# Delta-rule scan, then gated linear attention, each with projections between its steps, and softmax attention alone on four PSUM banks

## The chip, the cores and the metric

One core of a Trainium2 chip runs the whole kernel. The metric is device time in microseconds (us) of one execution.

## The reference, cut to what matters

Two layers of a latent-diffusion trunk on 512 latent and 256 context tokens (768 together), 1024 channels, fp32. In each layer three groups of heads read one input projection and write into one output projection, and a gated convolution FFN follows:

```python
pc = jnp.split(hc @ w_in, IN_SPLITS, axis=-1)
px = jnp.split(hx @ w_in, IN_SPLITS, axis=-1)
qn_x, qr_x, kn_x, kr_x, v_x = mla_project(px, mla_q_norm, mla_w_uq, mla_kv_norm, mla_w_ukv)
...
mla_x = mla_attention_blocked(qn_x, qr_x, cat(kn_c, kn_x), cat(kr_c, kr_x), cat(v_c, v_x))
gdn_c, gdn_x = bidirectional_scan(gated_delta_chunked, seq_c, dir_c, seq_x, dir_x, ...)
gla_c, gla_x = bidirectional_scan(gla_chunked, sq_c, dr_c, sq_x, dr_x, ...)
y_x = merge_heads(mla_x, gdn_x, z_x, gdn_norm, gla_x, gg_x, gla_norm) @ w_out
```

- MLA: softmax attention with 8 heads over keys and values that are projected up from a small rank.
- GDN, the gated delta rule: chunks of 64 tokens one after the other, 12 in each direction, with a state S per head. A step computes `v_new = u - w @ S`, `o = qd @ S + A @ v_new`, `S = S * glast + kend.T @ v_new`.
- GLA, gated linear attention: a short recurrence over chunk states, then an output for each chunk.

The second layer has no output for the context tokens.

## The kernel before, in words

fp32 products of the large matrices run as three products of high and low parts (`fprod`, `fsteps`, line 221: one step is three matmuls). Each engine's instructions have a fixed order, which the framework's scheduler writes when the kernel is built, from the order in which the Python code emits them. PSUM has eight banks: two tiles `bb` of two banks each (projections, scores of attention) and four single banks with the tags a, b, c and d. `ab("bc")` (line 183) hands out banks b and c in turn; `ab()` goes by `self.tags`. A tile of a bank must be read out before the next tile of that bank is written.

A layer emits, in this order (`layer`, line 310):

1. `project_in`: the part of w_in that GDN needs, and the preparation of each 128-token tile (`gdn_prep`, `gdn_tile`), with projection steps between, taken from a generator by `pace(n)` (line 232).
2. `gdn_scan` (line 970): 12 steps, both directions in one step. A step on TensorE: `kq` (keys and queries times the state Sb, 16 matmul records in the trace, line 990), then `vp` (line 1004), `up` (the update of the state, one bank for each direction, line 1015), `op` (line 1034). Between them on VectorE: r (996, 997), vs (1008), the four adds to Sb (1022), tq (1026), the output (1038 or 1041); vn on ScalarE (1029); Sb times its decay on GpSimd (1018). In steps 2, 3 and 8 to 11, where the other direction has already passed the chunk, the output of two chunks is complete, and `head_out` (line 1069) norms, transposes and gates it. All of it takes banks b and c in turn. `pace(8)` runs twice in a step, behind r and behind vp; the filler is the rest of the projections (`projections`: GLA's keys, queries and values, MLA's inputs, the gate), and its single banks are a and d. ada, the conditioning matmuls of the FFN's modulation, come from a background list.
3. `mla_project` (line 1251): keys, queries and V of MLA, banks a and d; then head pair 0 of attention.
4. `gla` (line 1085), banks c and d: the chunk states of both directions, seven levels for each segment of tokens (inside a chunk, lines 1187 to 1217), and an output for each 128-token tile (lines 1219 to 1248) with `head_out`. Context first, then latent; layer 1 needs no context output.
5. Attention of pairs 1 to 3 (line 1350), banks a and b. A tile of 128 queries and two heads: scores into `bb`, maximum (1377, VectorE), exponential (1380, ScalarE), transposes of P into single banks, copies out (1392, 1394), product with V in a single bank.
6. `w_out`, whose first matmuls need GLA's and GDN's rows of the mix (stored in `md`, read back at line 356), then the FFN.

The scheduler lets stages overlap in each engine's order as far as banks, buffers and data allow: before, attention's pair 0 runs while the scan ends, and GLA and attention's pairs run side by side.

Of the kernel before, what the change touches and what calls it, by code (L numbers as in the profile page):

```python
# [11 lines left out]
F32 = mybir.dt.float32  # L12
# [29 lines left out]
SN = (8, 8)  # L42
# [4 lines left out]
WO = ((4, 5, 6, 7, 0, 1, 2, 3), (4, 5, 6, 7, 0, 1, 2, 3))  # L47
SPF = 0
# [87 lines left out]
class Net:  # L136
# [40 lines left out]
    def s1(self, pool=None):  # L177
        return (pool or self.B).tile([128, 256], F32, name=self.nm("s"), tag="s", bufs=4 if pool is None else 6)
# [53 lines left out]
    def pace(self, n):  # L232

        while n and self.fill:
            try:
                next(self.fill[0])
                n -= 1
            except StopIteration:
                self.fill.pop(0)

# [70 lines left out]
    def layer(self, l, later):  # L311
# [16 lines left out]
        self.krope = self.dram([128, T], "krope")  # L328
        Fp, self.F = self.pool("F", "right")
        Cp, self.C = self.pool("C", "right")  # L330
        F1p, self.F1 = self.pool("F1", "right")
        F2p, self.F2 = self.pool("F2", "right")
# [4 lines left out]
        Ap, self.A = self.pool("A")  # L337
        A0p, self.A0 = self.pool("A0")
        A1p, A1 = self.pool("A1")
        with self.ahead(HM):  # L340
            self.mla_project(A1)
# [19 lines left out]
        self.tags = "ab"  # L361
# [191 lines left out]
    def project_in(self, later):  # L553
# [62 lines left out]
        def gdn(m):  # L616
            dst = dsts[m]
            for i in range(2):
# [3 lines left out]
                for a, b in segs:  # L622
# [7 lines left out]
                    if m != 1:  # L630
                        sq = self.F2.tile([128, 512], F32, name=self.nm("sq"), tag="sq", bufs=2)
# [7 lines left out]
        self.cq, self.ckv = [], []  # L639
        self.rr = self.small(12, "rr", 2)  # L640
# [48 lines left out]
        def projections():  # L689
# [3 lines left out]
            yield from gla_v()  # L693
            yield from mla_in(0)
            if not last:
                yield from mla_in(1)
            yield from gate(1)
# [22 lines left out]
        self.tags = "ad"  # L720
        self.gdn_scan()
        self.fill = []
        drain(rest)
# [246 lines left out]
    def gdn_scan(self):  # L970
# [7 lines left out]
        def s1():  # L978
            return self.s1(self.C)

        for n in range(12):
# [24 lines left out]
            self.pace(SN[1])  # L1006
            vs = s1()
            nc.vector.tensor_tensor(vs.rearrange(h4, h=4), vp[:, :256].rearrange(h4, h=4),
                                    self.eks[:, n].unsqueeze(2).to_broadcast(b4), op=ALU.mult)
            for d in range(2):  # L1010
                t, hf = ch[d] // 2, ch[d] % 2
                up = self.ab("bc")
# [10 lines left out]
            if need_o:  # L1023
                m = (3 if n < 4 else 15) - n
                vn, tq = s1(), s1()
                nc.vector.tensor_tensor(tq.rearrange(h4, h=4), ks[:, 256:].rearrange(h4, h=4), eg, op=ALU.mult)
                if m < n:
                    nc.gpsimd.tensor_tensor(tq, tq, ost[m], op=ALU.add)
                nc.scalar.copy(vn, vp[:, :256])
                op = self.ab("bc")  # L1030
                for h in range(4):
                    for d in range(2):
                        e = d * 4 + h
                        self.mm(op[half[d], h * 64:(h + 1) * 64], self.AT[ch[d] // 2][half[d], e * 64:(e + 1) * 64],
                                vn[half[d], h * 64:(h + 1) * 64], True, True)
                if m > n:
                    ost[n] = self.C.tile([128, 256], F32, name=self.nm("ost"), tag="ost", bufs=4)
                    nc.vector.tensor_tensor(ost[n], tq, op[:, :256], op=ALU.add)
                    continue

                nc.vector.tensor_tensor(tq, tq, op[:, :256], op=ALU.add)
                if n % 2 == 0:
                    lo = min(n, m) - 1
                    pieces = [(lo * 64, lo * 64 + 256)] if n < 10 else [(256, 384), (640, 768)]
                    zt = self.gates(0, pieces)
                first = (4 if n >= 10 else lo) if n % 2 == 0 else first
                pos = [c - first if c - first < 4 else c - first - 4 for c in (n, m)]
                self.head_out(tq, zt, [64 * pos[(hf - n) % 2] for hf in range(2)], 0)
                if n % 2:
                    self.ungates(zt, 0, pieces)  # L1050
# [16 lines left out]
    def head_out(self, o, zt, cols, i):  # L1067
# [8 lines left out]
        ps = self.ab("cd" if i else "bc")  # L1076
# [8 lines left out]
    def gla(self):  # L1085
# [11 lines left out]
        for a, b in (CS, XS):  # L1097
# [34 lines left out]
            for d in range(2):  # L1132
# [22 lines left out]
                for st in steps:  # L1155
# [30 lines left out]
            for li, w in enumerate((32, 16, 8, 4, 2, 1, 0)):  # L1186
# [21 lines left out]
                for x in range(2):  # L1208
# [3 lines left out]
                    for i in range(nt):  # L1212
                        for c in range(2):
# [3 lines left out]
                                              ps[:, :nt * 128].rearrange("p (e j) -> p e j", j=64))  # L1217

            for i in range(nt):
                t, sl = t0 + i, slice(i * 128, (i + 1) * 128)  # L1220
                pieces = [(a + i // 2 * 256, a + i // 2 * 256 + 256)]
                if i % 2 == 0:
                    zt = self.gates(1, pieces)
# [22 lines left out]
                self.head_out(o, zt, [p0, p0 + 64], 1)  # L1246
                if i % 2:
                    self.ungates(zt, 1, pieces)


    def mla_project(self, A1):
# [38 lines left out]
        for e in range(2):  # L1290
            rope = at("tab", 1)
            nc.sync.dma_start(rope, self.a["rope"][e])
            for p in range(4):
                wh, wl = self.wsplit(self.a["w_uq"][l, 2 * p + e], 384)
                ps = self.bb()
                self.fprod(ps, wh, wl, cqh, cql, self.osegs, 3)
# [10 lines left out]
        for t in range(6):  # L1307
# [8 lines left out]
            self.V.append(v)  # L1316

# [248 lines left out]
```

## Time and profile before

| | us |
|---|---|
| median of three runs | 2274.95 (2271.13 to 2276.51) |
| the profiled execution | 2278.35 |
| its span, first to last instruction | 2276.6 |
| TensorE busy in the span | 2045.0 (90%) |
| VectorE, ScalarE, GpSimd busy | 1310.4, 1008.7, 536.0 |
| granted TensorE clock, mean | 0.934 |

The median is the metric. The rows below are of the profiled execution, so a sum made from them is to be set against 2278.35 us. A granted clock of 1 is 2.4 GHz for TensorE, and half of it is 1.2 GHz; a mean of 0.934 says that TensorE ran at the lower level for a part of the time.

### The profile page before, as it was taken

How to read it: one execution, taken by the hardware profiler on the slowest of the kernel's cores; microseconds unless marked ns; L12 is line 12 of the kernel's file. 1: busy time of each engine (PE TensorE's matmuls, PEld its weight loads, DVE VectorE, ACT ScalarE, POOL GpSimd, SP SyncE). 2: the span in 40 equal slices, each digit the busy share in tenths (PEclk: the TensorE clock that was granted, in tenths of full speed). 3: DMA queues.
4: the chain of work that ended last, by engine and by line, in shares of the span. 5: the costliest groups of instructions: out<-in, count | busy, mean ns of one | idle time of the engine just before them, and what ended most of it. 6: DMA issues, size and time to landing. Idle time of an engine off the chain costs nothing. (4 is left out here: it accounts for less than half of the span.)

```text
span 2276.6 us, 44601 instructions
## 1 busy us (share of the span) xinstructions
PE 2045.0 (90%) x18168; PEld 1672.8 (73%) x18168; DVE 1310.4 (58%) x2474; ACT 1008.7 (44%) x1928; POOL 536.0 (24%) x897
## 2 busy tenths in 40 slices
PE   7898999888888799999999969988988777999996
PEld 4677777765667578888888857876766567888886
DVE  3354535668845743354454686556667757655556
ACT  4553323565464633332232456633446446543333
POOL 1342121135502310000010143413122613211102
PEclk8799999998898999999999979999989988999997
DMA  6232345422042354422212333111412053323322
GB/s 262 67 118 100 109 148 164 143 66 68 13 149 92 121 179 167 157 103 65 66 57 66 102 109 124 61 44 62 155 43 96 6 171 102 111 94 96 99 94 92
DMA packets 85134, 235.64 MB, mean 104 GB/s; under 512 B 9088, under 2 KB 24896, under 8 KB 84928
## 3 DMA queue, kind: packets, MB, share of 16 engines
q1 hardware_dynamic: 84928, 232.78, 30.7%
q8 instruction: 143, 2.34, 0.4%
q14 instruction: 63, 0.52, 0.1%
HBM read 204.04 MB, written 28.70 MB: 102 GB/s over the span
## 5 line engine op out<-in xcount | busy, mean ns | idle before, releaser
L212 PE MATMUL bb<-hh,wl 128*128 128x512 f32 (+1 forms) x1520 | 548.3, 361 | 18.0 <-DVE wl L192 10.9
L212 PE MATMUL bb<-hl,wh 128*128 128x512 f32 (+1 forms) x1520 | 542.0, 357 | 5.8 <-POOL hl L550 4.4
L192 DVE TENSOR_TENSOR wl<-wr,wh 128x512 fp32r<-128x512 f32 (+2 forms) x452 | 338.3, 751 | 362.3 <-ACT wh L191 361.0
L212 PE MATMUL bb<-hh,wh 128*128 128x512 f32 (+1 forms) x1520 | 540.2, 355 | 0.0
L191 ACT CAST wh<-wr 128x512 fp32r<-128x512 f32 (+2 forms) x452 | 274.1, 611 | 518.0 <-PE bb L212 370.3
L212 PEld LDWEIGHTS bb<-hh,wl 128*128 128x128 f32 x1520 | 293.2, 193 | 75.2 <-DVE wl L192 14.0
L212 PEld LDWEIGHTS bb<-hl,wh 128*128 128x128 f32 x1520 | 292.8, 193 | 49.4 <-POOL hl L550 7.8
L212 PEld LDWEIGHTS bb<-hh,wh 128*128 128x128 f32 x1520 | 292.9, 193 | 39.6 <-issue 2.1
L212 PE MATMUL bb<-g,wh 128*128 128x512 f32 (+1 forms) x1024 | 263.7, 349 | 2.3 <-DVE g L192 2.3
L1441 POOL TENSOR_SCALAR y<-u,fmt 128x512 f32<-128x512 f32 (+2 forms) x88 | 80.6, 917 | 527.1 <-ACT u L824 525.6
L212 PEld LDWEIGHTS bb<-g,wh 128*128 128x128 f32 x1024 | 181.5, 195 | 27.5 <-DVE g L192 3.3
L212 PE MATMUL bb<-g,wl 128*128 128x512 f32 (+1 forms) x512 | 180.3, 354 | 21.4 <-DVE wl L192 8.5
L212 PEld LDWEIGHTS bb<-g,wl 128*128 128x128 f32 x512 | 99.2, 195 | 36.9 <-ACT g L191 9.3
L824 ACT ACTIVATE u<-bb,fmt 128x512 f32<-128x512 f32 (+1 forms) x118 | 69.0, 613 | 85.0 <-PE bb L212 85.0
L212 PE MATMUL bb<-mh,wl 128*128 128x256 f32 (+1 forms) x256 | 85.2, 333 | 23.4 <-DVE wl L192 15.5
L1468 DVE TENSOR_TENSOR y<-y,bb 128x512 f32<-128x512 f32 (+2 forms) x80 | 54.8, 686 | 82.3 <-PE bb L212 82.2
L505 POOL TENSOR_TENSOR acc<-acc,sq 128x256 f32<-128x256 f32 (+1 forms) x48 | 49.5, 1031 | 183.9 <-ACT sq L503 180.9
L1442 DVE SCALAR_TENSOR_TENSOR y<-u,fmt,y 128x512 f32<-128x512 f32 (+2 forms) x88 | 72.3, 822 | 29.6 <-POOL y L1441 29.6
L212 PE MATMUL bb<-ml,wh 128*128 128x256 f32 (+1 forms) x256 | 84.1, 329 | 0.3
L1380 ACT ACTIVATE P<-bb,ast,srq 128x768 f32<-128x768 f32 (+1 forms) x80 | 72.6, 908 | 23.4 <-DVE ast L1378 14.5
L212 PE MATMUL bb<-mh,wh 128*128 128x256 f32 (+1 forms) x256 | 82.9, 324 | 0.0
L1377 DVE TENSOR_REDUCE ast<-bb 128x1 f32<-128x768 f32 (+1 forms) x80 | 67.2, 842 | 15.9 <-PE bb L212 15.6
(519 smaller groups left out, 3680.4 us busy)
## 6 DMA issues: line engine op xcount, KB each, us to landing
wr<-in_ffn_w_in SPq DMA_DIRECT2D x92, 512.0 KB, 3.5
wr<-in_w_ada SPq DMA_DIRECT2D x80, 512.0 KB, 3.9
wr<-in_ffn_w_out SPq DMA_DIRECT2D x48, 512.0 KB, 3.5
wr<-in_w_in SPq DMA_DIRECT2D x40, 512.0 KB, 4.3
wr<-in_w_out SPq DMA_DIRECT2D x32, 512.0 KB, 3.5
aw<-in_w_ada SPq DMA_DIRECT2D x16, 512.0 KB, 8.5
x<-in_xT SPq DMA_DIRECT2D x16, 384.0 KB, 8.7
wr<-in_w_uq SPq DMA_DIRECT2D x16, 192.0 KB, 2.6
```

The lines of the kernel that those rows point to most:

```text
L191: self.nc.scalar.copy(hi, src)
L192: (eng or self.nc.vector).tensor_tensor(lo, src, hi.bitcast(F32), op=ALU.subtract)
L212: self.nc.tensor.matmul(out, l, r, start=start, stop=stop)
L505: (nc.vector, nc.gpsimd)[k % 2].tensor_tensor(acc[k % 2], acc[k % 2], sq, op=ALU.add)
L824: nc.scalar.activation(u[:, a + o:b + o], ps[:, off + a:off + b], AF.Identity, bias=bias)
L1377: nc.vector.reduce_max(st[:, 0:1], sc, axis=AX)
L1380: nc.scalar.activation(P[:, :w], sc, AF.Exp, bias=st[:, 0:1], scale=self.srq[:, t:t + 1], accum_out=st[:, 1:2])
L1441: nc.gpsimd.tensor_scalar(yv, u[:, lo + 1:lo + 1 + n], cw[1], self.fm(P_FCB + i), op0=ALU.mult, op1=ALU.add)
L1442: nc.vector.scalar_tensor_tensor(yv, u[:, lo:lo + n], cw[0], yv, op0=ALU.mult, op1=ALU.add)
L1468: nc.vector.tensor_tensor(y, y, p, op=ALU.add)
```

## The change

The order of the stages, the pools that hold their buffers and the banks change. No matrix product is added or left out.

- The scan has one `pace(5)` behind each step in place of two `pace(8)` inside it. Its banks are fixed: key products and one direction's `up` in b, `vp` and the other's in c, query products and `op` together in d, the transposes of `head_out` in a, and `head_out` is put off by one step. tq is computed straight from bank d.
- When the scan is over, the rest of the projections and `mla_project` become a generator, `beside`, which GLA draws on with `pace` after every state step, level and output tile (`GN`). Their single banks are a and b.
- The gate projection comes ahead of MLA's inputs. `until` draws on the filler until GLA's inputs or its gate are there.
- Attention's pair 0 is emitted behind GLA, with banks a and b; pairs 1 to 3 get all of a, b, c and d.
- Pool F1 stays open till behind pair 0, F2 goes (its buffer moves to G), the scan has 8 small buffers in place of 6.

```diff
-SN = (8, 8)
+SN = 5
+GN = (8, 6, 5)
...
-        self.project_in(later)
-        for p in (self.Hp, F2p, F1p, Cp, Fp):
+        rest = self.project_in(later)
+        for p in (Cp, Fp):
             self.close(p)
...
+        def beside():
+            yield from rest
+            self.close(self.Hp)
...
+            yield from self.mla_project(self.A1)
+
+        self.tags = "ab"
+        self.fill = [beside()]
+        self.until("gla")
+        self.gla()
+        for g in self.fill:
+            drain(g)
...
         A2p, A2 = self.pool("A2")
-
-        with self.ahead(HA):
-            self.attention(A2, range(EP[l]))
-        with self.ahead(HG):
-            self.gla()
+        self.attention(A2, range(EP[l]))
+        self.close(A2p)
         self.close(Bp)
+        self.close(F1p)
+        A2p, A2 = self.pool("A2")
...
-        self.tags = "ab"
+        self.tags = "abcd"
         self.attention(A2, range(EP[l], 4), mh, ml, mixed)
...
         self.fill = [rest]
-        self.tags = "ad"
         self.gdn_scan()
-        self.fill = []
-        drain(rest)
+        return rest
...
-            ks = self.ab("bc")
-            for y in range(2 if need_o else 1):
-                for d in range(2):
-                    c = ch[d]
-                    for x in range(2):
-                        self.mm(ks[half[d], y * 256 + x * 128:y * 256 + x * 128 + 128],
-                                self.KQ[c // 2][:, x, y, half[d]], Sb[:, d, x], True, True)
+
+            ks = self.ab("b")
+            op = self.ab("d") if need_o else None
+            for y, z in ((0, ks), (1, op)):
+                if z is None:
+                    continue
+                for x in range(2):
+                    for d in range(2):
+                        self.mm(z[half[d], y * 256 + x * 128:y * 256 + x * 128 + 128],
+                                self.KQ[ch[d] // 2][:, x, y, half[d]], Sb[:, d, x], True, True)
...
-            self.pace(SN[0])
-            vp = self.ab("bc")
+            vp = self.ab("c")
...
-            self.pace(SN[1])
...
-                up = self.ab("bc")
+                up = self.ab("bc"[d])
...
+            for go in late:
+                go()
+            late = []
+            self.pace(SN)
...
-        ps = self.ab("cd" if i else "bc")
+        ps = self.ab("cd" if i else "a")
...
+                self.pace(GN[0] * nt // 4)
...
+                self.pace(GN[1] * nt // 4)
...
                 if i % 2 == 0:
+                    self.until("gate")
                     zt = self.gates(1, pieces)
...
+                self.pace(GN[2])
...
-            self.fprod(ps, wh, wl, kvh, kvl, XC, 2)
+            yield from self.fsteps(ps, wh, wl, kvh, kvl, XC, 2)
```

Three places of TensorE's order show what the build makes of this. The first is the middle of the scan in layer 0. Before, between `kq` (`Sb,kq`) and `up` (`s,ktok`) of a step, MLA's key projection runs (`kvh`, into a `bb` tile):

```order
L212 MATMUL c_4283<-Sb_3247,kq_2885 64x128 x2
L212 MATMUL bb_4751<-kvh_4676,wl_4748 128x512
L212 MATMUL bb_4751<-kvl_4678,wh_4747 128x512
...
L212 MATMUL bb_4774<-kvh_4676,wl_4771 128x512
L212 MATMUL bb_4774<-kvl_4678,wh_4770 128x512
...
L212 MATMUL bb_4774<-kvh_4677,wh_4770 128x256
L212 MATMUL b_4322<-s_4292,tt_2850 64x64
```

Now the steps of layer 0 stand one behind the other from the second step on, with `head_out`'s transposes (`cst,s`, bank a) and the ada matmuls (`wr,cTs`, also bank a) as the only others:

```order
L213 MATMUL d_3710<-Sb_3244,kq_2135 64x128
L213 MATMUL c_3725<-s_3719,tt_2100 64x64
...
L216 MATMUL a_3655<-cst,s_3535 128x128 x2
L213 MATMUL b_3739<-s_3734,ktok_450 64x64 x4
L213 MATMUL c_3747<-s_3734,ktok_450 64x64 x4
L213 MATMUL d_3710<-s_3736,at_1789 64x64
...
L213 MATMUL a_3677<-wr_3673,cTs 32x256 x4
L213 MATMUL a_3677<-wr_3675,cTs 32x256 x4
L213 MATMUL d_3710<-s_3736,at_2147 64x64
L213 MATMUL b_3781<-Sb_3244,kq_2493 64x128
```

What moved: the filler is gone from 312 of the 384 matmul entries of layer 0's scan (about 9.8 of 12 steps) and stands behind the scan. ada's tile `a_3677` comes behind the `head_out` tile `a_3655` of the same bank, and the weight loads of the next w_in tiles stand behind ada's in the same ring of three `wr` buffers.

The second place is the end of the scan in layer 1. Before, attention's pair 0 (`PT,V`, bank a) runs up to the last two steps:

```order
L212 MATMUL a_18512<-PT_18475,V_17510 64x128
L212 MATMUL a_18512<-PT_18501,V_17510 64x128
L212 MATMUL b_16969<-Sb_16403,kq_15340 64x128 x2
...
L215 MATMUL c_16963<-cst,s_16942 128x128 x2
L212 MATMUL c_16984<-s_16978,tt_15655 64x64
...
L212 MATMUL b_16995<-s_16993,ktok_13578 64x64 x4
L212 MATMUL c_17003<-s_16993,ktok_13578 64x64 x4
L212 MATMUL b_17016<-s_17011,at_15352 64x64
```

Now the last 6.75 steps stand alone (216 entries), and the V projection of MLA (`b_17794<-wh,kvl`), which pair 0 needs, comes behind the last of them, in bank b:

```order
L213 MATMUL d_16885<-s_16911,at_15699 64x64
L213 MATMUL b_16953<-Sb_16403,kq_15337 64x128
...
L213 MATMUL d_16954<-Sb_16403,kq_15337 64x128
...
L213 MATMUL c_16969<-s_16963,tt_15652 64x64
...
L216 MATMUL a_16948<-cst,s_16853 128x128 x2
L213 MATMUL b_16983<-s_16978,ktok_13575 64x64 x4
L213 MATMUL c_16991<-s_16978,ktok_13575 64x64 x4
L213 MATMUL d_16954<-s_16980,at_15349 64x64
...
L213 MATMUL d_17027<-s_17053,at_15010 64x64
L213 MATMUL b_17794<-wh_17786,kvl_17192 128x512
```

What moved: V's projection and the transposes of pair 0 left banks a and d for a and b, and b is the scan's. In a step, `op` and the query products now share bank d.

The third place is GLA's end in layer 1. Before, it follows attention's last tile (`dg,ones`), and the output projection's matmuls (`mh`, `ml`) follow its last `head_out`:

```order
L212 MATMUL b_19334<-dg_19321,ones 64x128
L212 MATMUL c_18209<-q_3028_18206,x_18199 64x128 x8
...
L212 MATMUL c_18259<-h_18253,h_18037 64x256 x2
...
L212 MATMUL c_18364<-gv_17817,A_18047 64x64 x8
L215 MATMUL d_18353<-cst,s_18343 128x128 x2
L215 MATMUL d_18387<-cst,s_18377 128x128 x2
L212 MATMUL bb_19416<-mh_18404,wl_19413 128x256
L212 MATMUL bb_19416<-ml_18412,wh_19412 128x256
```

Now the scores of pair 1 (`K`, `Q10l`) follow it:

```order
L213 MATMUL d_17950<-q_2878_17552,x_17938 64x128 x8
L213 MATMUL c_17968<-h_17962,h_17545 64x256 x2
...
L213 MATMUL c_18073<-gv_17115,A_17555 64x64 x8
L216 MATMUL d_18062<-cst,s_18052 128x128 x2
L216 MATMUL d_18096<-cst,s_18086 128x128 x2
L213 MATMUL bb_18460<-K_3081_18433,Q10l_18450 128x512
L213 MATMUL bb_18460<-K_3081_18433,Q10l_18450 128x256
```

What moved: pairs 1 to 3 stand behind GLA, whose last 192 entries (one direction's chunk states, seven levels, four output tiles) have nothing between them but `head_out`; at the end of the attention stage 48 matmul entries of the output projection stand among its last tiles (39 in layer 0).

## Rows read from the trace of the kernel before

**Rows 1.** Page, part 1: TensorE's busy time, share, instructions.

```profile
PE 2045.0 (90%) x18168; PEld 1672.8 (73%) x18168; DVE 1310.4 (58%) x2474; ACT 1008.7 (44%) x1928; POOL 536.0 (24%) x897
```

**Rows 2.** Windows: scan, then MLA, GLA and attention, in either layer (length; busy by engine; clock).

```profile
285.00:480.00 195.00, 177.97 (x1569) 143.84 (x1568) 106.65 (x242) 82.14 (x151) 38.25 (x52) 0.93 0.44 139
480.00:664.00 184.00, 153.35 (x1510) 112.95 (x1510) 132.46 (x332) 105.75 (x224) 80.14 (x113) 0.86 0.21 71
1581.00:1709.00 128.00, 107.39 (x1032) 84.30 (x1032) 86.19 (x200) 58.46 (x114) 27.05 (x44) 0.90 0.31 100
1709.00:1846.00 137.00, 105.69 (x1142) 80.44 (x1141) 94.50 (x216) 70.81 (x144) 50.29 (x68) 0.88 0.23 77
```

**Rows 3.** Windows: layer 0's filled scan, layer 1's filled scan, attention beside GLA.

```profile
288.00:424.00 136.00, 128.28 (x1133) 105.14 (x1132) 69.93 (x150) 44.03 (x82) 27.27 (x33) 0.95 0.54 172
1581.00:1640.00 59.00, 52.86 (x395) 40.93 (x397) 38.83 (x76) 22.26 (x42) 9.99 (x13) 0.94 0.52 170
1725.00:1750.00 25.00, 22.28 (x249) 17.10 (x249) 15.88 (x46) 15.11 (x36) 5.94 (x14) 1.00 0.47 158
```

**Rows 4.** Timeline, layer 1's last two scan steps, without filler (start, length, engine, line).

```profile
1689.87 1.09 PE L212 MATMUL b<-Sb,kq 128*64 128x128 f32 x16
...
1698.53 2.03 PE L212 MATMUL b<-Sb,kq 128*64 128x128 f32 x16 [0.58 <-DVE s L1041]
...
1700.60 0.42 DVE L996 TENSOR_TENSOR s<-b,egs 128x256 f32<-128x256 f32 x1 [0.36 <-PE b L212]
...
1701.06 0.47 DVE L997 TENSOR_TENSOR s<-s,s 128x256 f32<-128x256 f32 x1
...
1702.05 0.69 PE L215 MATMUL c<-cst,s 128*128 128x128 f32 x2 [1.49 <-POOL s L1075]
...
1703.41 1.12 PE L212 MATMUL c<-s,tt 64*64 64x64 f32 x16 [0.67 <-DVE zt L1082]
...
1705.38 0.37 PE L212 MATMUL b<-s,ktok 64*64 64x64 f32 x2 [0.85 <-DVE s L1026]
...
1705.77 0.42 PE L212 MATMUL c<-s,ktok 64*64 64x64 f32 x4
1706.19 0.58 DVE L1022 TENSOR_TENSOR Sb<-Sb,b 64x128 f32<-64x128 f32 x2 [0.86 <-POOL s L1028]
1706.80 0.58 DVE L1022 TENSOR_TENSOR Sb<-Sb,c 64x128 f32<-64x128 f32 x2
...
1708.14 0.42 DVE L1041 TENSOR_TENSOR s<-s,b 128x256 f32<-128x256 f32 x1 [0.76 <-PE b L212]
```

**Rows 5.** Timeline of TensorE, layer 1: attention's end, GLA's outputs, output projection.

```profile
1811.16 0.39 PE L212 MATMUL b<-dg,ones 128*64 128x128 f32 x4
...
1815.68 1.08 PE L212 MATMUL c<-h,h 128*64 128x256 f32 x8 [0.23 <-DVE A L1216]
...
1829.47 0.44 PE L215 MATMUL d<-cst,s 128*128 128x128 f32 x2 [2.52 <-POOL s L1075]
1836.39 0.58 PE L212 MATMUL bb<-mh,wl 128*128 128x256 f32 x1 [6.48 <-ACT mh L191]
...
1846.40 0.28 PE L212 MATMUL bb<-mh,wh 128*128 128x256 f32 x1
```

**Rows 6.** Groups by line and form, 1720 to 1832: GLA's levels.

```profile
L1207 POOL TENSOR_TENSOR q<-q,x 128x512 f32<-128x512 f32 x6 | 9.4, 1568 | 0.0
...
L1207 DVE TENSOR_TENSOR q<-q,x 128x512 f32<-128x512 f32 x6 | 6.4, 1067 | 0.1
...
L1216 DVE COPY_PREDICATED A<-cst,c 128x512 f32<-128x512 uint32 x7 | 5.1, 728 | 2.1 <-PE c L212 2.1
...
L1195 DVE TENSOR_TENSOR x<-h 128x256 f32<-128x256 f32 x6 | 3.3, 551 | 0.0
```

**Rows 7.** Timeline of TensorE, layer 1: scores of an attention tile, and three tiles later.

```profile
1721.50 0.62 PE L212 MATMUL bb<-K,Q00l 128*128 128x512 f32 x2
...
1743.34 0.62 PE L212 MATMUL bb<-K,Q00l 128*128 128x512 f32 x2
```

**Rows 8.** Groups by line and form, 1720 to 1832: attention's exponential and maximum.

```profile
L1380 ACT ACTIVATE P<-bb,ast,srq 128x768 f32<-128x768 f32 x18 | 17.9, 993 | 2.6 <-PE a L215 1.6 <-DVE ast L1378 0.9
L1377 DVE TENSOR_REDUCE ast<-bb 128x1 f32<-128x768 f32 x16 | 15.2, 949 | 3.8 <-PE bb L212 3.7
```

**Rows 9.** Timeline of TensorE, layer 0: the output projection's 39th matmul.

```profile
667.11 0.39 PE L212 MATMUL bb<-ml,wh 128*128 128x512 f32 x1
```

More of the change, by code (lines that the diff above doesn't have):

```diff
@@ L177, in s1 @@
     def s1(self, pool=None):
-        return (pool or self.B).tile([128, 256], F32, name=self.nm("s"), tag="s", bufs=4 if pool is None else 6)
+        return (pool or self.B).tile([128, 256], F32, name=self.nm("s"), tag="s", bufs=4 if pool is None else 8)
     def bb(self):
@@ L239, in pace, with until @@
                 self.fill.pop(0)
+    def until(self, what):
+        while what not in self.have:
+            self.pace(1)
     def rsqrt(self, out, ss, scale, bias):
@@ L328, in layer @@
         self.krope = self.dram([128, T], "krope")
+        F1p, self.F1 = self.pool("F1", "right")
         Fp, self.F = self.pool("F", "right")
         Cp, self.C = self.pool("C", "right")
-        F1p, self.F1 = self.pool("F1", "right")
-        F2p, self.F2 = self.pool("F2", "right")
-        self.project_in(later)
-        for p in (self.Hp, F2p, F1p, Cp, Fp):
+        rest = self.project_in(later)
+        for p in (Cp, Fp):
             self.close(p)
         Bp, self.B = self.pool("B", "right")
[L337 to L341, printed above, removed]
+        pools = []
+        def beside():
+            yield from rest
+            self.close(self.Hp)
+            for n in ("A", "A0", "A1"):
+                p, q = self.pool(n)
+                setattr(self, n, q)
+                pools.append(p)
+            yield from self.mla_project(self.A1)
[5 more added lines that the diff above has]
+            drain(g)
+        self.fill = []
+        Ap, A0p, A1p = pools
         self.close(A1p)
         A2p, A2 = self.pool("A2")
-        with self.ahead(HA):
-            self.attention(A2, range(EP[l]))
-        with self.ahead(HG):
-            self.gla()
+        self.attention(A2, range(EP[l]))
+        self.close(A2p)
         self.close(Bp)
+        self.close(F1p)
+        A2p, A2 = self.pool("A2")
         self.Xp, X = self.pool("X", "right")
@@ L630, in gdn @@
                     if m != 1:
-                        sq = self.F2.tile([128, 512], F32, name=self.nm("sq"), tag="sq", bufs=2)
+                        sq = self.G.tile([128, 512], F32, name=self.nm("sq"), tag="sq", bufs=2)
                         sqv = sq[:, :nt * 128]
@@ L639, in project_in @@
         self.cq, self.ckv = [], []
+        self.have = set()
         self.rr = self.small(12, "rr", 2)
@@ L693, in projections @@
             yield from gla_v()
+            self.have.add("gla")
+            yield from gate(1)
+            self.have.add("gate")
             yield from mla_in(0)
@@ L696, in projections @@
                 yield from mla_in(1)
-            yield from gate(1)
         if last:
@@ L979, in s1, with output, go @@
             return self.s1(self.C)
+        late = []
+        def output(n, tq, zt, cols, last):
+            def go():
+                self.head_out(tq, zt[0], cols, 0)
+                if last:
+                    self.ungates(*zt)
+            return go
         for n in range(12):
@@ L1035, in gdn_scan @@
                                 vn[half[d], h * 64:(h + 1) * 64], True, True)
+                nc.vector.tensor_tensor(tq.rearrange(h4, h=4), op[:, 256:].rearrange(h4, h=4), eg, op=ALU.mult)
                 if m > n:
@@ L1038, in gdn_scan @@
                     nc.vector.tensor_tensor(ost[n], tq, op[:, :256], op=ALU.add)
-                    continue
-                nc.vector.tensor_tensor(tq, tq, op[:, :256], op=ALU.add)
+                else:
+                    nc.vector.tensor_tensor(tq, tq, op[:, :256], op=ALU.add)
+                    nc.gpsimd.tensor_tensor(tq, tq, ost[m], op=ALU.add)
+            for go in late:
+                go()
+            late = []
+            self.pace(SN)
+            if need_o and m < n:
                 if n % 2 == 0:
@@ L1044, in gdn_scan @@
                     pieces = [(lo * 64, lo * 64 + 256)] if n < 10 else [(256, 384), (640, 768)]
-                    zt = self.gates(0, pieces)
-                first = (4 if n >= 10 else lo) if n % 2 == 0 else first
+                    zt = (self.gates(0, pieces), 0, pieces)
+                    first = 4 if n >= 10 else lo
                 pos = [c - first if c - first < 4 else c - first - 4 for c in (n, m)]
-                self.head_out(tq, zt, [64 * pos[(hf - n) % 2] for hf in range(2)], 0)
-                if n % 2:
-                    self.ungates(zt, 0, pieces)
+                late.append(output(n, tq, zt, [64 * pos[(hf - n) % 2] for hf in range(2)], n % 2))
+        for go in late:
+            go()
     def gates(self, i, pieces):
@@ L1295, in mla_project @@
                 ps = self.bb()
-                self.fprod(ps, wh, wl, cqh, cql, self.osegs, 3)
+                yield from self.fsteps(ps, wh, wl, cqh, cql, self.osegs, 3)
                 f = at("f", 2)
@@ L1316, in mla_project @@
             self.V.append(v)
+            yield
     def pair(self, pool, p):
```

9 lines of the change are left out of this document (3 added, 6 removed).

## The prediction, made before the changed kernel ran

> **What bounds the kernel now.** The page's first part comes first: TensorE is busy for 90% of the span [rows 1], so a gain has to come out of the other tenth, or out of time at the lower clock. Only the mixing stages of the two layers are touched, so the next view is that of windows over them [rows 2], 644 us in all. The reader is to see two losses in each row: TensorE idle (length less busy), 99.6 us over the four, and clock, (1 - clock) x length, 13.6 + 25.8 + 12.8 + 16.4 = 68.6 us. What is left, busy less the clock's part, I call work at full speed: 292 us in layer 0 (295 up to the output projection's 39th matmul at 667.1 [rows 9]), 184 in layer 1. No change of order can win more than 168 us here.
>
> The third view, windows of single stretches [rows 3], says where it is lost. Layer 0's scan with projections as filler does (128.28 - 0.05 x 136) / 136 = 0.89 of full-speed work, layer 1's 0.84, attention beside GLA 0.89 at clock 1.00. So filled stretches are good already, and the loss sits elsewhere: in the scan's unfilled end (the timeline [rows 4]: 8.66 us from one step's key products to the next, then 10.1, the 16 records taking 1.09 us at first and 2.03 later, which is the lower clock), and between attention's last matmul at 1811.16 and the output projection at 1836.39 [rows 5], 25 us with GLA's outputs and a wait of 6.5 us for their way through memory.
>
> **The change, part by part.** Work is conserved, so I share it out among new stages and divide each by a rate.
>
> *The preparation.* The first steps of layer 0's scan that lay inside it are fewer now, w_in matmuls more; a handful of microseconds of filler either way. Layer 0's preparation ends at 288 instead of 285: +3, and the work behind it is 292.
>
> *A scan step without filler.* The old step is a chain with detours: tq [line 1026] stands ahead of `up`, `head_out`'s transposes (bank c, waiting 1.49 us for GpSimd) ahead of vp, the output's read (1708.14) ahead of the next key products, since banks b and c go in turn. Fixed banks remove all three. What remains, by the rows at the lower clock [rows 4]: half of the key products 1.02 (r needs bank b alone), r 0.42, subtraction 0.47, vp 1.12, vs as r 0.42, `up` 0.81 (1705.38 to 1706.19), the four adds 1.19, and some 0.35 of hand-overs: 5.8 us. Query products and `op` run under r and under the adds; `head_out`, put off by a step, runs where TensorE waits for vs (0.69 against some 0.56). At the full clock the groups on TensorE shrink and the step is about 5.0; no row shows it, so that is the lower bound. The upper bound is the old step, 9.4 on the mean. I take 5.8, as most of the rows are the same instructions.
>
> *How many are unfilled.* By the order 9.8 steps in layer 0 and 6.75 in layer 1; before, the filler reached to the last two steps in layer 1 [rows 4]. A step holds about 2.8 us of full-speed work (1.09 for 16 records of the key products, a little over half of 1.12 for each of three other groups), so 16.5 steps x 5.8 = 96 us hold 46. That is a new loss of 50 us, 57 us of stage in layer 0 and 39 in layer 1. The gain has to come from what the displaced filler does later.
>
> *Attention of pairs 1 to 3 alone.* Three tiles begin 21.84 us apart [rows 7] in a stretch that is busy at 0.89 [rows 3]: 19.4 us, of which I put 2 down to GLA beside them (an estimate), so 5.8 a tile. ScalarE and VectorE have less to do: two exponentials of 0.99, two maxima of 0.95 a tile [rows 8] and copies, about 4 us each. With four single banks TensorE should be bound by itself; I take 0.9. Layer 0: 12 tiles of 5.8 and 6 context tiles of a third of the keys at 2.6 (estimate) = 85, and 39 output-projection matmuls 9: 94 / 0.9 = 104. Layer 1: 12 tiles and 48 short matmuls, 70 + 6 = 76, 83 us. Bounds of the rate: 0.76 (below) and 0.95.
>
> A rule of the Trainium skill speaks against this stage: "TensorE: Matmul & The Clock Gate", section "A second HAM failure mode: psum-queue depth-cycling", tells of a kernel that cycles through PSUM banks, idles shortly between groups, and swings between the clock's two levels. The row of attention on two banks in turn shows clock 1.00 with 11% idle, which does not agree; four banks in turn no row shows.
>
> *Layer 0's rest.* 292 - 27 (unfilled steps) - 94 = 171 us of work: two filled steps, the rest of w_in, MLA, GLA, pair 0, all interleaved. At the filled scan's 0.89 [rows 3] that is 192 us. The lower bound of the rate is that of MLA, GLA and attention before, (153.35 - 25.8) / 184 = 0.69 [rows 2].
>
> *Layer 1's rest.* GLA's end is alone: the second direction's chunk states, seven levels, four outputs. A level costs VectorE four products near 0.55, one of 1.07 and two copies of 0.73 [rows 6], 4.4 to 4.7 us, less for GpSimd (1.57 and one like it); 31 for seven, 3 for the states, 14 for the outputs (1815.68 to 1829.47 [rows 5]): 48 us for some 16 of work. What is left, 184 - 19 - 16 - 76 = 73, at layer 1's own filled rate of 0.84 [rows 3]: 87 us. In exchange GLA's results are long in memory when attention ends: the 25 us of [rows 5] go.
>
> *At nothing:* the tq read from the bank, fewer activation-table loads, gate and pool moves. ScalarE and VectorE have idle time beside TensorE in all rows of [rows 2]; without that cover they would be a few microseconds together. The DMAs of pairs 1 to 3 are issued behind pair 0's as before.
>
> *The sum.* Layer 0: 288 + 57 + 192 + 104 = 641 for 667.1: 26 won. Layer 1: from 1581, 39 + 87 + 48 + 83 = 257, so 1838 for 1846.4 [rows 5]: 8 won. Together 34 of the profiled execution's 2278.35: 2244. The runs' median lies 3.4 below that execution: 2241.
>
> **The rivals.**
> - *Slower: an unfilled step stays near the old one.* If the chain hangs on a bank again (bank d holds query products and `op`; its output is read about 0.25 us before the next query products want it) or on GpSimd, a step takes 9.4: 16.5 x 3.6 = 60 more, 2301. From 7.9 us a step (34 / 16.5 = 2.1 above mine) nothing is won. For it: the lower clock in [rows 4], which idle steps will keep. Against: all detours in those rows have a line that the change moves. Chance 0.17.
> - *GLA takes its filler badly.* Its levels are bound by VectorE [rows 6], and MLA's outputs also want VectorE and ScalarE. At 0.75 instead of 0.89 for the 143 us of layer 0's rest that lie behind the scan: 191 for 161, and about 7 more in layer 1: nothing is gained, about 2278. For it: 0.69 in that stage before; against: 0.89 beside attention. Chance 0.12.
> - *Attention alone loses the clock*, as the stage did on the mean before, 0.86 [rows 2]: rate 0.9 - 0.14 = 0.76, 124 for 104 and 100 for 83, 37 lost, 2278. Chance 0.08. The rule of the Trainium skill above would bring this about.
> - *More gained:* steps at 5.0 (-13), filled stages at 0.94 and 0.9 (-10, -6), attention at 0.95 (-10): 39 more, 2202. Chance 0.13.
>
> **How the numbers follow.** My forecast has 0.50, from 2215 to 2267. The two middle rivals spread about 2278, half inside 0.2% of before, which is about what a measurement of this kernel can tell from no change (4.6 us). Faster 0.65 (forecast and larger gain, and a little of the middle), same 0.11, slower 0.24 (the first rival and the rest). The range, 2203 to 2290, leaves out some of the largest gain and the greater part of the slow rival.
>
> **What would show it.** Right: key products 5.8 us apart in the unfilled steps at the lower clock, no wait for VectorE ahead of them but that for the adds to Sb; layer 0's scan over by 375, layer 1's by 1665; attention tiles alone some 6.4 us apart with clock near 1; the 39th output matmul near 641 in layer 0, the 48th near 1838 in layer 1. Wrong: steps above 7.9, or windows behind the scan that do less than 0.8 of full-speed work, or a low clock in attention alone. What I trust least is the 0.89 for GLA with projections between its steps, which no row shows.

## The result, and the profile after

The change makes the kernel slower: 2335.45 us (median, 2329.65 to 2339.63) beside 2273.04 for the kernel before on the same chip, ratio 1.0273 [1.0243, 1.0303]. The forecast was 2241, with a range up to 2290.

The profiled execution of after took 2337.6 us, its span is 2335.8. The page's part 1, which answers to [rows 1]:

```profile
PE 2046.7 (88%) x18168; PEld 1679.5 (72%) x18168; DVE 1319.1 (56%) x2474; ACT 1007.9 (43%) x1924; POOL 530.6 (23%) x897
```

TensorE does the same 18168 records in 1.7 us more, while the span is 59.2 longer: 57.5 us are idle time. Where the time lies is read from the last TensorE matmul of each stage in the two traces (a row whose stage "ends with" a first matmul, from that one). Each number of this table is the time from one such mark to the next; the last two columns are those of the best experiment, x13_all_mo.

| stage ends with | before | after | diff. | x13 | diff. |
|---|---|---|---|---|---|
| last preparation matmul, layer 0 | 282.4 | 287.4 | +5.0 | 278.8 | -3.6 |
| last output-projection matmul (mixing, layer 0) | 463.6 | 468.8 | +5.2 | 444.8 | -18.8 |
| last FFN matmul | 600.9 | 603.7 | +2.8 | 600.3 | -0.6 |
| **first preparation matmul, layer 1** | 105.1 | 127.9 | **+22.8** | 104.9 | -0.2 |
| last preparation matmul, layer 1 | 126.9 | 128.2 | +1.3 | 128.9 | +2.0 |
| last output-projection matmul (mixing, layer 1) | 319.3 | 343.0 | **+23.7** | 314.0 | -5.3 |
| last FFN matmul | 362.2 | 362.1 | -0.1 | 364.9 | +2.7 |

The fourth row is a place of which the prediction does not speak at all. The forecast for the mixing stages was -26 and -8, at marks a little ahead of the table's. The 39th matmul of layer 0's output projection came 13.0 us late (680.1 for 667.1 before) and was forecast 26 early; from layer 1's last preparation matmul to the 48th it took 20.8 us more (288.3 for 267.5) and was forecast 8 less. The first row lies between 278 and 293 us over all experiments, so a difference of a few us in one row is not traced to a cause here.

Windows of after show what the new order made of the stages (start:end, length, then busy time of PE, PEld, DVE, ACT and POOL; TensorE's clock, DMA share, GB/s). They answer to [rows 2, 3]:

```profile
290.00:372.00 82.00, 64.77 (x866) 48.56 (x862) 45.35 (x130) 21.26 (x52) 23.70 (x35) 0.96 0.17 61
374.00:560.00 186.00, 159.38 (x1427) 124.98 (x1428) 129.84 (x266) 83.28 (x156) 77.66 (x97) 0.88 0.37 123
560.00:600.00 40.00, 19.85 (x121) 16.22 (x119) 23.87 (x40) 22.57 (x34) 1.86 (x5) 0.66 0.56 204
600.00:682.00 82.00, 78.49 (x682) 63.25 (x682) 49.63 (x143) 53.39 (x127) 11.98 (x31) 1.00 0.17 52
1672.00:1698.00 26.00, 19.76 (x342) 14.32 (x345) 18.33 (x55) 7.55 (x21) 9.60 (x15) 1.00 0.01 2
1760.00:1810.00 50.00, 25.53 (x278) 19.11 (x274) 25.94 (x52) 10.37 (x18) 23.37 (x26) 0.64 0.02 6
1810.00:1830.00 20.00, 6.22 (x19) 4.86 (x20) 13.05 (x20) 12.36 (x19) 0.37 (x1) 0.50 0.74 257
1850.00:1906.00 56.00, 55.13 (x494) 44.66 (x490) 33.65 (x89) 33.95 (x71) 7.15 (x17) 1.00 0.20 65
```

The unfilled scan (first and fifth row) and attention on four banks (fourth and eighth) came out as forecast or better, GLA alone in layer 1 (sixth) some 8 us over. The second row, GLA with filler, did not: busy less the clock's part, 159.38 - 0.12 x 186, is 137 us of full-speed work in 186, a rate of 0.74. And between GLA and pair 1 there are two stretches of which the forecast knew nothing (third and seventh row): TensorE half or two thirds idle, its mean clock 0.66 and 0.50, with the DMA engines busy.

**Three hand-overs of memory.** A hand-over is a place where a buffer lies over an older one: its first writer has to wait until the older one has been read or stored for the last time. After has idle time at three of them, and the experiments below test each. The first is the start of layer 1. The timeline of after (the bracket is the idle time before an instruction and what ended it):

```profile
1373.46 0.39 PE L213 MATMUL bb<-hh,wh 128*128 128x512 f32 x1
...
1388.17 1.93 PE L213 MATMUL c<-ones,acc 128*128 128x1 f32 x8 [9.84 <-DVE acc L524]
...
1398.40 0.10 POOL L836 MEMSET u<- 128x2 f32 x1
1398.47 0.56 ACT L842 COPY u<-bb 128x512 f32<-128x512 f32 x1
1399.09 0.79 PE L213 MATMUL bb<-hh,wl 128*128 128x512 f32 x1 [7.15 <-ACT u L842]
```

and of x5_funder, where F lies below F1 as before:

```profile
1349.70 0.09 POOL L837 MEMSET u<- 128x2 f32 x1
...
1362.63 0.57 ACT L843 COPY u<-bb 128x512 f32<-128x512 f32 x1
```

The projections ran on to 1373.46, then both `bb` tiles were full. `u`, the convolution's input in pool F1, takes the first of them; its memset on GpSimd came at 1398.40, when the residual and its norm (`acc`) were through. The change opens F1 first on the right side (that line of its diff is not among those shown above), and by the order in which the pools are opened and closed F1 lies on the residual's own buffers. In x5, with F opened first as before, the memset ran at 1349.70 and the copy at 1362.63.

The second is the start of GLA. DMA issues and TensorE in after, layer 1 (the scan's last matmul is at 1698.5):

```profile
1707.64 0.42 SPq L1140 DMA_DIRECT2D h<-gkd x1
...
1721.91 0.38 PE L216 MATMUL c<-cst,h 128*128 128x128 f32 x2
```

GLA's pool lies over the scan's pools F and C. Its loads go out 9 us after the scan, its first matmul runs 23 us after it (31 in layer 0). In x5 the same load goes out at 1654.20, before the scan's end.

The third lies between GLA and pair 1 (timeline of after, both layers):

```profile
568.85 3.27 ACT L192 CAST K<-wr 64x768 fp32r<-64x768 f32 x4 [2.12 <-DMA mix<-mo]
574.60 0.98 PE L213 MATMUL bb<-K,Q10l 128*128 128x512 f32 x2 [14.32 <-DVE Q10l L193]
...
1812.07 3.27 ACT L192 CAST K<-wr 64x768 fp32r<-64x768 f32 x4 [4.66 <-DMA md<-zt]
...
1816.75 0.69 DVE L193 TENSOR_TENSOR Q10l<-wr,Q10h 128x512 fp32r<-128x512 f32 x1
...
1817.55 0.98 PE L213 MATMUL bb<-K,Q10l 128*128 128x512 f32 x2 [8.75 <-DMA ml<-mix]
```

A2 is closed and opened again behind pair 0. Pair 1's keys now lie over buffers of pair 0 and GLA, so their split on ScalarE waits for the stores out of them (`mix<-mo`, `md<-zt`), and TensorE waits for the splits of keys and queries. (In layer 1 the bracket names the load `ml<-mix` beside it; the split of Q10l ends at 1817.44, 0.1 us before the matmul.)

### The profile page after: what moved, and what is told of

The parts are those of the page before. It is cut to its first block, busy times and chain, and to the rows that moved or that the text cites. A ratio compares the mean times of both kernels' runs of the same rounds, so it can differ in the third digit from the quotient of the medians.

```text
span 2335.8 us, 44688 instructions
## 1 busy us (share of the span) xinstructions
PE 2046.7 (88%) x18168; PEld 1679.5 (72%) x18168; DVE 1319.1 (56%) x2474; ACT 1007.9 (43%) x1924; POOL 530.6 (23%) x897
## 4 chain that ended last, share of the span: by engine, by line
PE 61%; DVE 12%; ACT 5%; DMA 5%; issue 4%; POOL 2%; SPq 0%; DVEq 0%; ACTq 0%; POOLq 0%
PE bb L213 49%; PE c L213 3%; PE b L213 3%; PE d L213 3%; DVE y L550 2%; PE a L213 2%; DVE wl L193 1%; DMA wr<-in_w_in 1%; PE a L216 1%; ACT wh L192 1%; PE b L216 1%; DVE Sb L1055 1%; DMA wr<-in_ffn_w_in 1%; PE d L216 1%; DMA mix<-mo 1%
## 5 line engine op out<-in xcount | busy, mean ns | idle before, releaser
L844 ACT ACTIVATE u<-bb,fmt 128x512 f32<-128x512 f32 (+1 forms) x118 | 68.9, 613 | 82.5 <-PE bb L213 82.5
L1416 DVE TENSOR_REDUCE ast<-bb 128x1 f32<-128x768 f32 (+1 forms) x80 | 67.6, 848 | 29.4 <-PE bb L213 23.7
L1422 POOL TENSOR_SCALAR dg<-cst,ast 128x128 f32<-128x128 f32 x80 | 31.8, 399 | 228.0 <-DVE ast L1420 131.3
```

The costliest lines, as they stand in the source:

```text
L844: nc.scalar.activation(u[:, a + o:b + o], ps[:, off + a:off + b], AF.Identity, bias=bias)
L1416: nc.vector.reduce_max(st[:, 0:1], sc, axis=AX)
```

## The experiments

The time of the kernel before beside each run was 2273 to 2278 us. "Stages" means the rows of the table above.

**F1 on the other side (x1, x2).**

```diff
-        F1p, self.F1 = self.pool("F1", "right")
+        F1p, self.F1 = self.pool("F1")
...
             yield from rest
+            self.close(F1p)
...
-        self.close(F1p)
```

> The pool F1 (buffers of the projections) lies on the other side of memory and is closed when the projections end, nothing else changed. First theory: the loss against before is lost at two places where memory, not work, is waited for: the convolution's buffers at the start of layer 1 (they lie where the residual was: some 25 us), and pair 1's keys and queries, whose buffers are free only when GLA's are (some 20 us in either layer). F1's place causes both, so this kernel takes about 55 to 65 us less than the change: 2270 to 2285 us, near before. Rival: attention on four banks has to wait for GLA's banks c and d anyway, so the hole between GLA and pair 1 stays and only the start of layer 1 comes back: about 2310 us.

Measured: 2337.35, ratio 1.0267 [1.023, 1.0305]. Neither theory held. The start of layer 1 stayed at 129.1; I put that down to the FFN's buffers on the left, which are read late as well (argued from the order of the pools; no run separates it). The time from GLA's last product (`gv,A`) to attention's last matmul was 133.7 in layer 0 (132.9 in after), and in layer 1 it fell from 100.1 to 83.2. x2 puts an empty buffer of F1's size beneath GLA's:

> As x1_f1left, but with an empty buffer of F1's size held beside GLA's buffers, so that pair 1's keys and queries find no memory before GLA's end, as in the change; only the start of layer 1 is mended. First theory: layer 1's preparation begins some 25 us earlier against the end of layer 0 and the holes behind GLA stay: about 2310 us. If this kernel is as slow as the change (2335), the start of layer 1 is not lost to F1's place; if it is as fast as x1_f1left, the holes behind GLA don't come from memory.

Measured: 2343.11, 1.0301 [1.0257, 1.0345]. About the start of layer 1 this says nothing (129.6), as x1 had not mended it; but layer 1's time behind GLA was back at 100.6: it goes by where the buffers lie.

**Pair 1 on two banks, and the bank of `head_out` (x3, x4).** x3 is x1 with `self.tags = "ab"` for pair 1; x4 is x1 with the scan's `head_out` in bank c in place of a, so that projections need not queue behind it for a bank.

> As x1_f1left, but pair 1 of attention uses banks a and b alone, pairs 2 and 3 all four. First theory: GLA's unfilled end in layer 1 (50 us, TensorE busy for half of it at a clock of 0.64) then has pair 1 beside it, which brings 15 to 25 us against x1_f1left: 2250 to 2265. Rival: GLA's end is bound by VectorE, which attention needs as well, so pair 1 only slows it: within 5 us of x1_f1left.

> As x1_f1left, but the scan's head_out takes bank c in place of a, so that ada's matmuls (bank a) and behind them the weight loads of the projections no longer wait for the scan's end: layer 0's scan is filled for 7 of 12 steps. First theory: the filler that is done beside the scan is missing behind it, where GLA with projections ran at 0.74 of full-speed work and not at 0.89, and the low clock goes: 8 to 15 us less than x1_f1left. Rival: head_out's bank is waited for by vp and a scan step gets longer by 0.5 to 1 us: no gain or a few us lost.

Measured: x3 2326.33, 1.0232 [1.0198, 1.0266]: 11 us less than x1, neither the 15 to 25 of the theory nor the rival's 5; by the stages it has 11 less in layer 1's mixing and 13 more in layer 0's. x4 2324.42, 1.0212 [1.0179, 1.0246]: 13 less than x1, as its theory said; by the stages 9 less in layer 0's mixing and 6 more in layer 1's. The four runs of x1 lie 15 us apart, so both gains are little above the noise. Neither mends the slowdown.

**F below F1, and GLA's buffers from F (x5), F1 lowest again (x12).** In x5, F is opened first and kept until pair 0 is through; GLA takes its small tiles, its states and `gv` from F's tags, which the scan has done with one after the other, and has two buffers in place of four for its outputs. The edit, cut:

```diff
-        F1p, self.F1 = self.pool("F1", "right")
         Fp, self.F = self.pool("F", "right")
+        F1p, self.F1 = self.pool("F1", "right")
...
-        for p in (Cp, Fp):
-            self.close(p)
+        self.close(Cp)
...
-        return self.B.tile([128, 512], F32, name=self.nm("h"), tag="h", bufs=HB)
+        return self.F.tile([128, 512], F32, name=self.nm("h"), tag=("kq", "tt", "at")[n % 3], bufs=6)
...
```

> The change with its pools in another place: F below F1 in memory, kept until GLA's end, and GLA's buffers taken from F's (2 small buffers in place of 4 for its outputs). x1_f1left did not bring back the start of layer 1: there F1 lay where the FFN's own buffers are read to the last. Theory: it is the place of the convolution's buffers after all; here it is over buffers of the FFN that come free early, as before, so from the end of layer 0's FFN to layer 1's first preparation matmul it takes some 105 us and not 128, and the kernel about 2310 us. Rival: the start of layer 1 is late for another reason (the order of ScalarE's and GpSimd's instructions): 128 us there, 2335 in all.

Measured: 2289.57, 1.0064 [1.0044, 1.0085]. The start of layer 1 is 106.7 and GLA begins 1.5 us behind the scan (1.7 in layer 1); this is 46 us under after, more than expected. x12 separates the two: x5 with F1 opened ahead of F.

> x5_funder with F1 lowest again, as in the change: GLA's buffers still come out of F's, so GLA can begin at the scan's end, but the convolution's buffers lie over the residual's. Separates the two halves of x5_funder's 46 us: if the start of layer 1 and GLA's begin are two losses, layer 0's FFN to layer 1's preparation takes some 128 us again, GLA begins within 3 us of the scan's end as in x5_funder, and the kernel takes 20 to 30 us more than x5_funder, about 2315. Rival: both came from one cause, and this kernel is as x5_funder (2290) or as the change (2335).

Measured: 2323.32, 1.0206 [1.0179, 1.0233]; start of layer 1 127.6, GLA still 1.5 us behind the scan. The two are separate losses: F1's place costs 33.8 us (x12 less x5; 20 to 30 expected), 20.9 of them at the start of layer 1 and 14.3 in layer 0's preparation, and GLA's pool 12.1 (after less x12; the other buffer counts of GLA are in this figure). GLA was 23 to 31 us late, but projections ran meanwhile.

**The kernel before with F1 lowest (x6).** F1 opened first, as in the change, in the kernel before; the order of closing follows.

```diff
+        F1p, self.F1 = self.pool("F1", "right")
         Fp, self.F = self.pool("F", "right")
         Cp, self.C = self.pool("C", "right")
-        F1p, self.F1 = self.pool("F1", "right")
...
-        for p in (self.Hp, F2p, F1p, Cp, Fp):
+        for p in (self.Hp, F2p, Cp, Fp, F1p):
```

> The kernel before with one edit of the change alone: the pool F1 is opened first and so lies lowest, over the residual's buffers of the layer ahead. Theory of the place: 20 to 25 us slower than before, all of it between layer 0's FFN and layer 1's preparation: about 2297 us. Rival: as before, within 5 us.

Measured: 2306.36, 1.0131 [1.0109, 1.0154]; the start of layer 1 grows by 21.9, layer 0's preparation by 5.6. Timeline of x6, where before has this copy at 1361.45:

```profile
1376.67 0.56 ACT L822 COPY u<-bb 128x512 f32<-128x512 f32 x1
```

An edit that only places a buffer, with the old order of stages, costs 33 us by the medians (20 to 25 expected; 25.6 between the two profiled executions, where these two rows stand for 27.5). The new order of scan, GLA and attention is not its cause.

**A2 not closed (x7, x8).** x7 is x1 without closing and reopening A2; x8 is x7 with `head_out` in bank c.

> As x1_f1left, but pair 0's pool is not closed before pair 1, so that pair 1's keys and queries have memory of their own and can come in while GLA and pair 0 still run, in both layers; attention keeps four banks. Theory: the hole of 14 us behind pair 0 in layer 0 and the half-filled 10 us after it go: 12 to 20 us less than x1_f1left, 2317 to 2325. Rival: the hole is one of banks, and nothing changes.

> x7_keepa2 with head_out of the scan in bank c, as in x4_hoc. If the hole and the blocked filler are separate losses they add up: 10 to 15 us less than x7_keepa2 (2305 to 2312). If both are the same loss seen from two sides (less work left behind the scan), x8 is as x4_hoc, 2324.

Measured: x7 2308.65, 1.0149 [1.0124, 1.0174], 29 us under x1 where 12 to 20 were expected: the time behind GLA falls from 133.7 to 109.1 in layer 0. x8 2336.41, 1.0259 [1.0235, 1.0283], which neither theory had: 28 us worse where x4 had gained 13.

**All three mended (x9), and two questions put to it (x10, x11).** x9 is x5 with a pool of its own for pair 1's keys and queries, opened ahead of pair 0 and filled behind it; for the room, pair 0 has two buffers of P and of PT in place of four, and GLA's outputs come out of F's tags too. The edit, cut:

```diff
+        A3p, self.A3 = self.pool("A3")
         A2p, A2 = self.pool("A2")
+        self.pb = 2
         self.attention(A2, range(EP[l]))
+        self.pair(self.A3, 1)
         self.close(A2p)
...
```

> x5_funder (F below F1, GLA's buffers out of F), and pair 1's keys and queries in a pool of their own that is there before GLA ends (pair 0 has two buffers of P and PT in place of four to make room). Theory: three hand-overs of memory cost what the change lost, and each is mended apart: layer 0 to 1 and scan to GLA (x5_funder, 2290), GLA to pair 1 (x7_keepa2: 17 us in layer 0, 17 in layer 1 by x5_funder's hole there). Together 2250 to 2262 us, faster than before. Rival: with the holes gone TensorE waits for VectorE and ScalarE instead, and no more than 10 us of the 34 come back: 2280.

Measured: 2263.52, 0.9948 [0.993, 0.9965]. Faster than before, by 0.5%, 1.5 us above the expected 2250 to 2262, and 72 us under after: 12.1 and 33.8 as above, 26.1 for this step. Of the 26.1, the two mixing stages show 12.5 and 4.6 between the traces of x5 and x9; the rest lies in stages that the edit leaves alone, and is not explained. x10 gives pairs 1 to 3 two banks in place of four, x11 puts `head_out` into bank c.

> x9_all with attention of pairs 1 to 3 on banks a and b as before, in place of four. If four banks are what fills attention (98% busy in the change, 6 us a tile), two cost 5 to 10%: 8 to 15 us more than x9_all. If the absence of other work is what fills it, no difference.

> x9_all with head_out of the scan in bank c, so that filler runs beside 7 of layer 0's 12 scan steps and less is left behind it. The change's own blocked filler would be a loss if this gains 5 us or more; x4_hoc gained 13 on x1_f1left and x8_keepa2_hoc lost 28 on x7_keepa2, so the sign is open. If filler only changes places, as TensorE's work is the same, within 5 us of x9_all.

Measured: x10 2290.08, 1.0066 [1.004, 1.0093], 27 us worse: attention needs the four banks, and more than I expected. With two, and the hand-overs of x9 mended, the new order is slower than before, so its gain hangs on the four. x11 2284.14, 1.0052 [1.0029, 1.0075], 21 us worse, which neither theory had: filler held up in the scan is not where gain is missing.

**Pair 0's output out of the reopened pool (x13).** x9 still has a piece of the third hole in layer 0. Its timeline, and the line that x13 changes:

```profile
562.31 0.99 ACT L1423 ACTIVATE P<-bb,ast,srq 128x768 f32<-128x768 f32 x1 [2.98 <-DMA mix<-mo]
...
563.45 1.11 PE L217 MATMUL c<-cst,P 128*128 128x128 f32 x4 [8.97 <-ACT P L1423]
```

```diff
-            mo = at("mo", MOB)
+            mo = self.A3.tile([128, T], F32, name=self.nm("mo"), tag="mo", bufs=MOB)
```

> The kernel with all three hand-overs mended still has a hole in layer 0 behind pair 0: its profile shows TensorE waiting 8.97 us at 563.45 for the first exponential of pair 1, whose buffer of P in the reopened pool A2 waits until 562.31 for the store of pair 0's output out of the old A2 (DMA mix<-mo), and the window 556 to 571 runs at clock 0.56. Here pair 0's output lies in pair 1's own pool, so nothing in the reopened pool waits for that store. If the store is what holds pair 1, the wait at its first transposes falls to under 4 us, layer 0's attention alone falls from 118 to 105-112 us, and the time to 2250-2259 us. The rival says that ScalarE's casts of the mix rows (mh<-ml), which stand ahead of that exponential and wait for their loads, are what holds it: then the wait stays at 6 us or more and the time at 2261-2266 us.

Measured: 2254.02, 0.9907 [0.9884, 0.993], and the wait fell to 1.85 us, as the theory said. The store it was. In the timeline of x13:

```profile
551.71 1.11 PE L217 MATMUL c<-cst,P 128*128 128x128 f32 x4 [1.85 <-ACT P L1423]
```

and in its windows, GLA with filler and attention in layer 0 (pair 0 ends at 549.6 there), and attention in layer 1:

```profile
369.00:536.00 167.00, 145.66 (x1351) 113.28 (x1350) 120.51 (x250) 77.42 (x138) 73.45 (x85) 0.90 0.42 140
536.00:647.00 111.00, 101.88 (x866) 82.13 (x868) 70.49 (x194) 75.76 (x172) 16.16 (x42) 0.98 0.29 102
...
1735.00:1819.00 84.00, 76.25 (x658) 62.48 (x660) 50.26 (x126) 52.75 (x105) 11.53 (x25) 0.92 0.28 89
```

The hand-overs had hidden a gain of 0.9%. One more is left in x13, in layer 1: TensorE waits 7.17 us at 1743.22 for pair 1's first exponential, ahead of which ScalarE waits for a store of GLA's output (`md<-zt`). No run mends that one.

## Why the prediction was wrong

**The step that failed** is the one under "At nothing": "gate and pool moves", with "The DMAs of pairs 1 to 3 are issued behind pair 0's as before". I took the change's pools as a matter of room. They decide which instruction must have read or stored an address before another may write it. By the runs, F1's place cost 33.8 us, most of it in a stage that I had not looked at; GLA's pool 12.1; pair 1's keys 26.1 (with what x9 changed beside them), and the store of pair 0's output 9.5 more (x9 less x13). The DMAs of pair 1 do stand behind pair 0's, but the splits behind them waited for stores that the old order had long behind it. My rival on the slow side was another mechanism.

**An unfilled step, 5.8 us:** the chain was right, its clock was not, and the size was a little high. Timeline of after, three steps of layer 1, which answer to [rows 4]:

```profile
1678.25 0.43 PE L213 MATMUL b<-Sb,kq 128*64 128x128 f32 x2
1678.86 0.62 PE L213 MATMUL b<-Sb,kq 128*64 128x128 f32 x6 [0.18 <-DVE Sb L1055]
...
1683.06 0.43 PE L213 MATMUL b<-Sb,kq 128*64 128x128 f32 x2
1683.67 0.62 PE L213 MATMUL b<-Sb,kq 128*64 128x128 f32 x6 [0.18 <-DVE Sb L1055]
...
1688.14 0.43 PE L213 MATMUL b<-Sb,kq 128*64 128x128 f32 x2
```

They are 4.8 and 5.1 us apart, at full clock where the forecast had the lower one, and the only wait at a step's start is the one for the adds to Sb. So they came out at the lower bound of 5.0. By the prediction's own terms that bound was too high: with TensorE's part of the 5.8 (1.02, 1.12 and 0.81) halved, the sum is 4.3 (an estimate). Layer 0's scan was over at 371.7 (forecast 375), layer 1's 82.5 us behind its preparation (forecast 84, from 1581 to 1665). The rival of slow steps fell.

**Attention alone:** right in its rate once pair 1 is under way: TensorE is busy for 98% of 1850 to 1906 at clock 1.00. In x13, layer 0's pairs 1 to 3 take 97.7 us from pair 0's last matmul on (549.6 to 647.3; forecast 104), and layer 1's 83.7 from GLA's last transposes on (1735.6 to 1819.3; forecast 83, though 76 / 0.9 is 84). The second match is in part luck: the window has 76.25 - 0.08 x 84 = 69.5 us of full-speed work at a rate of 0.83, where the forecast has 76 at 0.9. The rival of a lost clock fell too. The rule of the Trainium skill ("TensorE: Matmul & The Clock Gate", section "A second HAM failure mode: psum-queue depth-cycling") was weighed with this stage. The trace does not show its swings, as cycling through four banks kept the clock at 1.00; but at 98% busy there is little of the short idling between groups that the rule also names, so it is not refuted by this.

**GLA with filler at 0.89:** mis-sized, as I had said of it that I trusted it least. Behind the scan the forecast has 162 us (375 to 537) in layer 0, until GLA and pair 0 are through. From the scan's end to pair 0's last matmul after took 188 (371.7 to 560.0) and x13 182 (367.5 to 549.6), at (145.66 - 0.10 x 167) / 167 = 0.77 of full-speed work by its window up to GLA's end. The sign that the prediction named, less than 0.8 behind the scan, did come. So the second rival's rate, 0.75, was nearer than mine. In x13 these 20 us are in part made up by an earlier scan's end (7.5) and shorter attention (6). No single wait explains it: in x9 the longest sum of one releaser in this stretch is 3.4 us (GpSimd's `h`), and in x13 VectorE is busy for 72% of it (120.51 of 167). That these chains set the rate is argued, not shown.

**GLA alone in layer 1, 48 us:** in after it is 56, from pair 0's last matmul (1753) to the end of GLA's last transposes (1808.8). The outputs took 15 us for 14, but the seven levels 39 (1754 to 1794) for 31: in one place, at 1773.22, TensorE waited 11.79 us for GpSimd's `q`, which stood behind 9.12 us of products for the outputs on that engine. The forecast priced the levels by VectorE alone, with "less for GpSimd".

**The sum:** with these hand-overs mended (x13), and by the forecast's own marks, the 39th output matmul of layer 0 comes 20.7 us earlier (646.4) where 26 were forecast, and layer 1's 48th 7.8 us sooner behind its preparation (259.7 for 267.5) where 8 were. The whole gains some 21 us (0.93% of before's time) where 34 were forecast. What stays open is the sign of `head_out`'s bank: c gained 13 us in x4 and lost 28 in x8 and 21 in x11.

## What to carry to other kernels

When a change opens, closes or reorders pools, write down for each new buffer which old one it lies on, who reads or stores that last, and what then waits behind the first write on its engine; look beyond the stages whose order changes, up to the next layer. A wait whose releaser is a store, or another stage's instruction that does not make the operand, is a likely hand-over: give the buffer a place whose last reader is early, and the order that looked bad may turn out good.

## What the hardware showed that I had not expected

In after the unfilled scan of layer 1 kept the full clock. Before, the last two steps with TensorE busy for 10.1 of 18 us (1690 to 1708) ran at a mean of 0.60, as [rows 4] show in their 2.03 us for the key products; after, with 19.76 of 26 us busy (1672 to 1698), the clock was 1.00. There the chain with the detours removed gained twice: by the waits and by the clock. It does not always: in x13, 300 to 310 of layer 0's scan ran at 0.56 with TensorE busy for 8.74 of 10 us, and the steps around it (293.9 to 312.4) took 5.4, 7.1 and 6.0 us. No run here shows what made the difference. In the hole of after behind GLA, 1810 to 1830 (6.22 of 20 us busy), the clock was 0.50.
